# A diffusion trunk layer in fp32: part of a matrix product moved to VectorE, and a new order in the attention

## Chip, cores and metric

One core of a Trainium2 chip. The metric is the device time of one launch in microseconds; lower is better. Engines: TensorE (PE), VectorE (DVE), ScalarE (ACT), GpSimd (POOL), and SyncE (SP), which only issues loads and stores here.

## What is computed

One layer (DEPTH is 1) on 128 context tokens and 256 latent tokens, width 2048, all fp32:

```python
m = silu(cond) @ w_mod + b_mod          # six rows of 2048 for each of two conditions
h = rms_norm(x, n1) * (1 + sc1) + sh1
q, k, v, u = split(h @ w_in)            # 16 heads of 64, and a Fourier part u
attn = softmax(q k^T / 8 + bias) v      # neighbourhood window and context keys
fn = real(fft2(u))                      # over positions and group channels
g_na, g_fn = split(sigmoid(h @ w_gate))
x = x + g1 * ((g_na * (attn @ w_na) + g_fn * (fn @ w_fnet)) @ w_o)
h2 = rms_norm(x, n2) * (1 + sc2) + sh2
x = x + g2 * swiglu(h2, w_gate_up, w_down)
```

Context tokens use the condition c_ctx, latent tokens c. The outputs are both token sets and the context's k and v.

## The kernel before

Every large product is made of three matmuls (mm3, L147 to L149): each fp32 operand is split into a high part H, rounded to fp32r, and a low rest L, and H·H, H·L and L·H are added in PSUM. Weights come in units of 256 rows by 512 columns (load_unit, L185, on SP's queue; four buffers). split_unit (L195) makes wh on ScalarE and wl on VectorE, one unit ahead of PE. The program's order is written out by hand: the units are a fixed list, and next_unit (L208) lets the front work make a step (A), splits the next unit, lets the front and the other work make a step (B), and issues the load of a later unit. In the gate stage, mid_unit makes a third step for the front work halfway through the unit's matmuls (M). A Paced generator (L58) collects its rate at each tick and makes its steps when what it has collected reaches `least`. Ahead (L84) issues loads some items before their use; loads on SP's queue go out in program order, and one that waits for its buffer holds up those behind it.

The stages are these. First the tokens' norm and transposes. Then the projection by w_in, in four groups of k-tiles (GROUPS: k-tile 0, then 1 and 2, then 3 to 6, then 7 to 15), each group running over eight column chunks: 8, 8, 16 and 40 units. Beside it, prepare (L570) computes shift and scale of the first norm for the k-tiles of MODS (one, then five times three): mod_sums (L392) multiplies the 32 columns of csz, of which two hold the conditions, with 128 rows of w_mod at a time (wm, L384, two k-rows a load, four buffers); four such matmuls at column positions 0, 32, 64 and 96 are one step. mod_cols (L416) turns the sums into columns, and modulate (L535) makes the tokens hH and hL of a k-tile. When prepare is through, the stream `rows` starts (with_rows, L605): mod_rows (L306) adds up w_mod's other four parts on VectorE (accr, L329), sums over partitions on PE (L338) into a PSUM bank, and adds the bank to the bias row one step later (L343).

Next is the gate projection, eight times eight units, with the Fourier mix (fourier, L697) and then the attention (L802) as front work, and with `rows`. The Fourier mix calls positions for each group and half, splits the next u, and calls channels. The attention goes pair of heads by pair; the string PAIR gives the calls of each tick, by the table at L992: t0 and t1 transpose probabilities, qk transposes q and k, b adds the mask, lq, lb and lv load, s0 and s1 are the scores, m0 and m1 their maxima, e0 and e1 the exponentials on ScalarE with their sums, i0 and i1 (inverses, L939) the reciprocals on VectorE and the scaling on ScalarE (L944), pv the values, v a split of the values. All of these share the four PSUM banks of at_tile with `rows`; a bank is given again when its last reader has been written into the program. The gate products use the four others.

Then come the two branch projections with the gates (f4, L1081), the output projection (cc, L1170), in which transposed (L1151) makes the next product's operand from finished columns, and the feed-forward part in six rounds.

Of the kernel before, what the change touches and what calls it, by code (L numbers as in the profile page):

```python
# [13 lines left out]
F32 = mybir.dt.float32  # L14
# [5 lines left out]
P = 128  # L20
# [19 lines left out]
GROUPS = [(0, 1), (1, 2), (3, 4), (7, 9)]  # L40
ORDER = [6, 7, 0, 1, 2, 3, 4, 5]
DUE = [-1.4, 0, 0, 0]
PREP = [1.75, 1.8, 1.8, 1.8]
PAIR = "t1 qk,b,,,,lq,s0 s1 m0,e0 i0,m1,pv lb,e1 i1,,t0,v,lv"

# [54 lines left out]
def trunk_kernel(ctx: ExitStack, tc: tile.TileContext, io: dict):  # L102
# [163 lines left out]
    with ExitStack() as ph:  # L266
# [22 lines left out]


        ROWS = (2, 4, 3, 5)

        def row_weights():

# [11 lines left out]
        def mod_rows(ty, src):  # L306


            for cc in range(2):
                acc = rpool.tile([P, 2, 2, CH], F32, tag="acc", name=nm("accr"))  # L310
                row = rpool.tile([P, CH], F32, tag="row", name=nm("row"))
                nc.gpsimd.memset(row, 0.0)
                b = b_mod[ty * D + cc * 2 * CH : ty * D + (cc + 1) * 2 * CH].rearrange("(i n) -> i n", i=2)
                for cnd in range(2):
                    for i in range(2):
                        q = 64 * cnd + 32 * i
                        nc.gpsimd.dma_start(row[q : q + 1], b[i : i + 1])
                for k in range(KT):
                    _, wm = src.take()
                    for cnd in range(2):  # L320
                        if cnd:
                            if ty != ROWS[0] or cc + k:
                                src.more()
                            yield
                        sc = csz[:, k, cnd : cnd + 1]
                        if k == 0:
                            nc.vector.tensor_scalar_mul(acc[:, cnd], wm, sc)
                        else:
                            nc.vector.scalar_tensor_tensor(  # L329
                                out=acc[:, cnd], in0=wm, scalar=sc, in1=acc[:, cnd], op0=ALU.mult, op1=ALU.add  # L330
                            )
                    yield
                yield
                o = rows_psum["tile"]()
                for cnd in range(2):
                    for i in range(2):
                        q = 64 * cnd + 32 * i
                        nc.tensor.matmul(  # L338
                            o[q : q + 32], ones, acc[:, cnd, i], start=True, stop=True,
                            tile_position=(0, q), skip_group_check=True,  # L340
                        )
                yield
                nc.vector.tensor_add(row, row, o)  # L343
                for cnd in range(2):
                    for i in range(2):
                        q = 64 * cnd + 32 * i
                        c0 = (2 * cc + i) * CH
                        nc.gpsimd.dma_start(s_row[ty][cnd][:, c0 : c0 + CH], row[q : q + 1])
# [23 lines left out]
        def depth_of(n):  # L372

            return 4 if n == 1 else 2

        def mod_weights(alloc):


            def load(kt0, n, k0):
                w, nk = n * P, depth_of(n)  # L380
                wm = alloc([P, 2, nk, w], "wm")
                for ty in range(2):
                    col = ty * D + kt0 * P
                    nc.sync.dma_start(  # L384
                        wm[:, ty],
                        w_mod[k0 * P : (k0 + nk) * P, col : col + w].rearrange("(k p) n -> p k n", p=P),
                    )
                return wm

            return Ahead(load, [(kt0, n, k0) for kt0, n in MODS for k0 in range(0, KT, depth_of(n))], 0)  # L390

        def mod_sums(src, kt0, n, alloc, out):  # L392

# [3 lines left out]
            for k0 in range(0, KT, nk):  # L397
                _, wm = src.take()
                for kk in range(0, nk, 2):
# [13 lines left out]
                        out.append(rows)  # L413
                    yield

        def mod_cols(kt0, n, rows):  # L416

            pt = md_tile()
            for j in range(n):
                nc.tensor.matmul(pt[:, j * 4 : j * 4 + 4], rows[:, j * P : (j + 1) * P], sel, start=True, stop=True)  # L420
            m = pt[:, : n * 4].rearrange("p (k i c) -> p k i c", i=2, c=2)
            yield


            def bc(ap):
                return ap.unsqueeze(2).to_broadcast([P, n, 2])

            nc.vector.tensor_add(msh[0][:, kt0 : kt0 + n, :], m[:, :, 0], bc(bcol[:, kt0 : kt0 + n]))
            d = msc[0][:, kt0 : kt0 + n, :]
            nc.vector.tensor_add(d, m[:, :, 1], bc(bcol[:, KT + kt0 : KT + kt0 + n]))  # L430
            nc.vector.scalar_tensor_tensor(
                out=d, in0=d, scalar=1.0, in1=bc(ng[:, 0, kt0 : kt0 + n]), op0=ALU.add, op1=ALU.mult
            )
            yield


        with ExitStack() as pha:
            wmp = phm.enter_context(tc.tile_pool(name="wmp", bufs=4, side="right"))
            cpool = pha.enter_context(tc.tile_pool(name="cpool", bufs=12))
            tmp = pha.enter_context(tc.tile_pool(name="tmpa", bufs=2))  # L440

# [15 lines left out]
                nc.sync.dma_start(t[:, 0, :], xp[:, cc * CH : (cc + 1) * CH])  # L457
                xc.append(t)
            src = mod_weights(wme)
            for _ in range(2):  # L460
                src.more()
            loads = Ahead(load_unit, units, 1)
            for _ in range(2):
                src.more()
            loads.more()

            rows_n = tmp.tile([64, P], F32, tag="rows_n", bufs=1, name="rows_n")
            nc.gpsimd.dma_start(rows_n[0:16], io["norm1_g"][0].rearrange("(k p) -> k p", p=P))
# [101 lines left out]
            def prepare():  # L570

                follow = columns_and_tokens(*MODS[0])
                while prepared[0] < 1:
                    yield next(follow)
                for k0, n in MODS[1:]:
                    for _ in mod_sums(src, k0, n, wme, sums):
                        next(follow, None)
                        yield
                    follow = columns_and_tokens(k0, n)
                    while k0 == 1 and prepared[0] < 3:  # L580
                        yield next(follow)
                for _ in follow:
                    yield

            prep = Paced(prepare())
            rows_psum["tile"] = md_tile

            def rows_and_columns():
# [62 lines left out]

            for gi, (k0, n) in enumerate(GROUPS):
                prep.due, prep.rate = DUE[gi], PREP[gi]
                prep.least = 3.6 if gi else 1
                if gi == len(GROUPS) - 1:
                    behind.append(Paced(expand_rpb(), 0.2))
                    new_ring()
# [39 lines left out]
        def fourier():  # L697
            with ExitStack() as st:
# [8 lines left out]
                def split_table(name, raw):  # L707
                    H, L = (fc.tile(raw.shape, F32R, tag=name + x, name=nm(name + x)) for x in "HL")
                    split(H, L, raw)
                    return H, L  # L710

                def load_u(g):
                    return table([P, NT, FG], s_qkvu[6 + g // 2][:, :, (g % 2) * FG : (g % 2 + 1) * FG])
# [64 lines left out]
                for pair in range(2):  # L778
                    for gi in range(2):
                        for cc in range(2):  # L780
                            positions(gi, cc)
                            yield
                            if pair + gi + cc == 0:
                                chH, chL = split_table("chan", chan)
                            yield
                        if pair + gi < 2:
                            uH, uL = split_table("u", u)
                            yield
                            if pair == 0:
                                u = load_u(gi + 2)  # L790
                        yield
                    if pair:
                        for got, load in ((qks, load_qk), (biases, load_bias), (vs, load_v)):
                            got.append(Ahead(load, [(hp,) for hp in range(8)], 1))
                    for cp in range(2):
                        channels(pair, cp)
                        yield
                        yield
                        yield
# [48 lines left out]
        def attention_pair(hp, wk, rest):  # L848
# [90 lines left out]
            def inverses(qt):  # L939
                sm = t["sm", qt]  # L940
                n = len(halves[qt])
                nc.vector.reciprocal(sm[:, :n], sm[:, :n])
                for i, (j, sl) in enumerate(halves[qt]):
                    nc.scalar.activation(  # L944
                        out=sc[:, j, sl], in_=sc[:, j, sl], func=AF.Copy, scale=sm[:, i : i + 1]
                    )

            def keys_first(qt):

# [198 lines left out]
        rows_until(2)  # L1148
        yield from load_rows(tmpo, 2, cc, "gb", 2)

    def transposed(cc, tile=at_tile):  # L1151

        for k in range(4):
            kt = cc * 4 + k
# [7 lines left out]
            for g, sl in conds:  # L1162
                nc.vector.scalar_tensor_tensor(
                    out=L[:, sl], in0=o[:, sl], scalar=g, in1=fr(H[:, sl]), op0=ALU.mult, op1=ALU.subtract
                )
            yield

    rows.rate = RATES[3]
    xin = [None] * 4
    for cc in range(4):  # L1170
# [3 lines left out]
        for u in range(0, KT, 2):  # L1174
# [7 lines left out]
                shifts(xw, 0)  # L1182
            if u == 2 and cc:
                rows_until(4)
                behind.append(Paced(transposed(cc - 1)))
            for t in range(NT):
                sl = slice(t * P, (t + 1) * P)
                for kk in range(2):
# [55 lines left out]
            yield  # L1244

    norm = Paced(normed(), 1.25, 3)
    behind += [Paced(inverse()), Paced(transposed(3, mm_tile), 1, 1), norm]


    phf = ctx.enter_context(ExitStack())  # L1250
# [162 lines left out]
```

## Time and profile before

| | |
|---|---|
| three runs | 2046.58, 2047.31, 2047.31 us; median 2047.31 |
| the profiled execution | 2046.09 us, span 2044.3 us |
| PE busy | 2022.1 us, 99% |
| VectorE busy | 1244.4 us, 61% |
| ScalarE busy | 758.6 us, 37% |
| DMA over the span | 192 GB/s |
| granted PE clock, mean | 0.997 |

A busy engine is not always at its peak: matmuls are pipelined and their ends are modelled, so PE's share says that the stream has hardly a hole, and the distance from one start to the next says how dense it is. The span is that of the profiled execution; its time is 1.8 us longer, and the median of the runs another 1.2 us.

### The profile page before, as it was taken

To read this page: it belongs to the slowest core of one execution; us is meant where nothing else is said; L and a number is where in the kernel's file an instruction comes from. 1 tells how busy PE (TensorE), PEld (TensorE's weight loads), DVE (VectorE), ACT (ScalarE), POOL (GpSimd) and SP (SyncE) were. 2 spreads that over 40 slices of the span, in tenths; PEclk is the share of its full clock that TensorE was granted. 3 is DMA by queue.
4 is the path that set the end of the run, shared out by engine and by line. 5 is a ranking of instruction groups with operands and counts; after the bars stand their busy time and mean duration, and the time that the engine had idled before them with its cause. 6 is when DMAs were issued, how large, how long until landed. Compare 5 with 4: busy or idle time off the path is not lost.

```text
span 2044.3 us, 27532 instructions
## 1 busy us (share of the span) xinstructions
PE 2022.1 (99%) x10986; PEld 1844.3 (90%) x10986; DVE 1244.4 (61%) x1524; ACT 758.6 (37%) x1139; POOL 43.0 (2%) x92
## 2 busy tenths in 40 slices
PE   7999999999999999999999999999999999999999
PEld 4668888999999999889998999899989998999897
DVE  4746898778988778765844454544454334333456
ACT  5433232456656443334523332222322232323222
POOL 1000000000000000010000000000000000000000
PEclk8999999999999999999999999999999999999999
DMA  9995979677776776754455455444554444444453
GB/s 328 334 338 181 330 261 323 206 224 225 230 209 185 251 245 200 240 189 139 120 169 162 147 156 160 148 155 148 162 155 141 124 127 125 132 124 125 138 161 124
DMA packets 220384, 390.46 MB, mean 191 GB/s; under 512 B 28464, under 2 KB 77632, under 8 KB 220256
## 3 DMA queue, kind: packets, MB, share of 16 engines
q1 hardware_dynamic: 213088, 382.13, 59.5%
q10 hardware_dynamic: 4672, 6.31, 0.8%
q8 instruction: 86, 1.41, 0.3%
q0 software_dynamic: 2496, 0.27, 0.1%
q14 instruction: 42, 0.34, 0.0%
HBM read 371.81 MB, written 20.51 MB: 192 GB/s over the span
## 4 chain that ended last, share of the span: by engine, by line
PE 93%; DMA 3%; DVE 2%; ACT 1%; issue 0%; SPq 0%; ACTq 0%; DVEq 0%
PE mm L147 19%; PE mm L149 19%; PE mm L148 19%; PE at L147 11%; PE at L149 11%; PE at L148 11%; PE at L404 1%; DVE wl L144 1%; DMA wm<-in_w_mod 1%; DMA wraw<-in_w_in 1%; DVE accr L329 1%; DMA xc<-in_x_prompt 0%; PE at L981 0%; PE at L960 0%; PE at L338 0%
## 5 line engine op out<-in xcount | busy, mean ns | idle before, releaser
L144 DVE TENSOR_TENSOR wl<-wraw,wh 128x1024 fp32r<-128x1024 f32 (+1 forms) x464 | 559.1, 1205 | 672.7 <-ACT wh L143 668.9
L143 ACT CAST wh<-wraw 128x1024 fp32r<-128x1024 f32 (+1 forms) x464 | 481.1, 1038 | 1036.8 <-PE at L148 274.1
L147 PE MATMUL mm<-hH,wh 128*128 128x384 f32 x1152 | 387.9, 337 | 0.2 <-ACT gst L1036 0.2
L149 PE MATMUL mm<-hH,wl 128*128 128x384 f32 x1152 | 385.3, 334 | 0.0
L148 PE MATMUL mm<-hL,wh 128*128 128x384 f32 x1152 | 385.2, 334 | 0.0
L329 DVE SCALAR_TENSOR_TENSOR accr<-wmr,csz,accr 128x1024 f32<-128x1024 f32 x240 | 304.2, 1278 | 0.1
L147 PEld LDWEIGHTS mm<-hH,wh 128*128 128x128 f32 x1152 | 216.3, 188 | 5.1 <-issue 4.5
L148 PEld LDWEIGHTS mm<-hL,wh 128*128 128x128 f32 x1152 | 216.3, 188 | 0.0
L149 PEld LDWEIGHTS mm<-hH,wl 128*128 128x128 f32 x1152 | 216.2, 188 | 0.0
L147 PE MATMUL at<-hH,wh 128*128 128x384 f32 x640 | 213.9, 334 | 0.0
L149 PE MATMUL at<-hH,wl 128*128 128x384 f32 x640 | 213.9, 334 | 0.0
L148 PE MATMUL at<-hL,wh 128*128 128x384 f32 x640 | 213.8, 334 | 0.0
L147 PE MATMUL mm<-wh,hH 128*128 128x512 f32 x404 | 160.8, 398 | 1.9 <-ACT hH L548 1.2
L149 PE MATMUL mm<-wh,hL 128*128 128x512 f32 x404 | 158.4, 392 | 0.6 <-DVE hL L144 0.4
L148 PE MATMUL mm<-wl,hH 128*128 128x512 f32 x404 | 158.0, 391 | 0.8 <-DVE wl L144 0.8
L149 PE MATMUL mm<-wh,cL 128*128 128x512 f32 x352 | 137.1, 389 | 0.0
L147 PE MATMUL mm<-wh,cH 128*128 128x512 f32 x352 | 137.0, 389 | 0.0
L148 PE MATMUL mm<-wl,cH 128*128 128x512 f32 x352 | 137.0, 389 | 0.0
L147 PEld LDWEIGHTS at<-hH,wh 128*128 128x128 f32 x640 | 120.1, 188 | 1.0 <-ACT wh L143 0.8
L148 PEld LDWEIGHTS at<-hL,wh 128*128 128x128 f32 x640 | 120.1, 188 | 0.2
L149 PEld LDWEIGHTS at<-hH,wl 128*128 128x128 f32 x640 | 120.1, 188 | 0.0
L147 PEld LDWEIGHTS mm<-wh,hH 128*128 128x128 f32 x404 | 76.1, 188 | 25.6 <-issue 3.1
(282 smaller groups left out, 2631.1 us busy)
## 6 DMA issues: line engine op xcount, KB each, us to landing
wraw<-in_w_gate_up SPq DMA_DIRECT2D x176, 512.0 KB, 3.7
wmr<-in_w_mod SPq DMA_DIRECT2D x128, 512.0 KB, 4.9
wraw<-in_w_down SPq DMA_DIRECT2D x88, 512.0 KB, 3.7
wraw<-in_w_gate SPq DMA_DIRECT2D x64, 512.0 KB, 4.3
wm<-in_w_mod SPq DMA_DIRECT2D x80, 384.0 KB, 6.8
wraw<-in_w_in SPq DMA_DIRECT2D x56, 512.0 KB, 6.2
wraw<-in_w_o SPq DMA_DIRECT2D x32, 512.0 KB, 4.6
wraw<-in_w_fnet_proj SPq DMA_DIRECT2D x16, 512.0 KB, 5.0
```

The source lines that it names most:

```text
L143: nc.scalar.copy(H, x)
L144: nc.vector.tensor_sub(L, x, fr(H))
L147: nc.tensor.matmul(out, aH, bH, start=start, stop=False)
L148: nc.tensor.matmul(out, aH, bL, start=False, stop=False)
L149: nc.tensor.matmul(out, aL, bH, start=False, stop=stop)
L329: nc.vector.scalar_tensor_tensor(out=acc[:, cnd], in0=wm, scalar=sc, in1=acc[:, cnd], op0=ALU.mult, op1=ALU.add)
L404: nc.tensor.matmul(pm[q : q + 32, :w], csz[:, k, :], wm[:, ty, kk + par, :], start=k < 2, stop=k >= KT - 2, tile_position=(0, q), skip_gro ...
```

## The change

The modulations of the last three k-tiles (13 to 15) are computed in two ways. For the first four of 16 k-rows (EARLY) they stay on PE. For the other twelve, late_sums loads 128x384 pieces (wd, five buffers) and adds them up on VectorE, for each condition, in tiles that later hold the tokens of k-tiles 13 and 14; it is paced at 1.5 pieces a unit from the second group on. late_rows then makes the first four k-rows' matmuls and four matmuls with `hot`, whose column of ones sums each accumulator over the partitions into its row of the same bank. prepare's rates in the last two groups fall to 1.6. At the start, all four first wm loads go out ahead of the two w_in units.

In mod_rows, ScalarE copies the sums out of the bank in the tick of its matmuls, and VectorE adds the copy. In the Fourier mix, both halves of a group are called in one tick, the split of the next u follows one tick later, and a group of ticks is one longer. In the attention, i0 and i1 come two ticks after their exponentials, and VectorE does the scaling. In the output projection, transposed does two k-tiles a step at half the rate.

```diff
-PREP = [1.75, 1.8, 1.8, 1.8]
-PAIR = "t1 qk,b,,,,lq,s0 s1 m0,e0 i0,m1,pv lb,e1 i1,,t0,v,lv"
+PREP = [1.75, 1.8, 1.6, 1.6]
+LATE = 1.5
+EARLY = 4
+PAIR = "t1 qk,b,,,,lq,s0 s1 m0,e0,m1,i0 pv lb,e1,,i1 t0,v,lv"
...
+        hot = consts.tile([P, 2, 32], F32, tag="hot", name="hot")
+        nc.vector.memset(hot, 0.0)
+        for cnd in range(2):
+            nc.vector.memset(hot[:, cnd, cnd : cnd + 1], 1.0)
...
+                nc.scalar.copy(acc[:, 0, 0], o)
                 yield
-                nc.vector.tensor_add(row, row, o)
+                nc.vector.tensor_add(row, row, acc[:, 0, 0])
...
+            got = Ahead(load, [(k, ty) for k in range(EARLY, KT) for ty in range(2)], 5)
+            yield
+            for k in range(EARLY, KT):
+                for ty in range(2):
+                    if k + ty > EARLY:
+                        got.more()
+                    _, wd = got.take()
+                    for a, sc in zip(late_acc[ty], (csz[:, k, cnd : cnd + 1] for cnd in range(2))):
+                        if k == EARLY:
+                            nc.vector.tensor_scalar_mul(a, wd, sc)
+                        else:
+                            nc.vector.scalar_tensor_tensor(
+                                out=a, in0=wd, scalar=sc, in1=a, op0=ALU.mult, op1=ALU.add
+                            )
+                    yield
...
+            for ty in range(2):
+                for cnd, a in enumerate(late_acc[ty]):
+                    q = 32 * (2 * ty + cnd)
+                    nc.tensor.matmul(
+                        pm[q : q + 32, :w], hot[:, cnd], a, start=False, stop=True,
+                        tile_position=(0, q), skip_group_check=True,
+                    )
...
-            for _ in range(2):
+            for _ in range(4):
                 src.more()
-            loads = Ahead(load_unit, units, 1)
-            for _ in range(2):
-                src.more()
-            loads.more()
+            loads = Ahead(load_unit, units, 2)
...
-                for k0, n in MODS[1:]:
+                for k0, n in MODS[1:-1]:
...
-                for _ in follow:
+                prep.least = 1
+                yield from follow
+                while late.live:
+                    late.step()
                     yield
+                late_rows(*MODS[-1], wme, sums)
+                yield
+                yield from columns_and_tokens(*MODS[-1])
...
-                prep.least = 3.6 if gi else 1
+                prep.least = 3.6 if gi in (1, 2) else 1
+                if gi == 1:
+                    behind.append(late)
...
                         for cc in range(2):
                             positions(gi, cc)
-                            yield
-                            if pair + gi + cc == 0:
-                                chH, chL = split_table("chan", chan)
-                            yield
+                        yield
                         if pair + gi < 2:
                             uH, uL = split_table("u", u)
+                        yield
+                        if pair + gi == 0:
+                            chH, chL = split_table("chan", chan)
+                        yield
+                        if pair == 0:
+                            u = load_u(gi + 2)
+                        for _ in range(3):
                             yield
-                            if pair == 0:
-                                u = load_u(gi + 2)
-                        yield
...
-                    nc.scalar.activation(
-                        out=sc[:, j, sl], in_=sc[:, j, sl], func=AF.Copy, scale=sm[:, i : i + 1]
-                    )
+                    nc.vector.tensor_scalar_mul(sc[:, j, sl], sc[:, j, sl], sm[:, i : i + 1])
...
-    def transposed(cc, tile=at_tile):
+    def transposed(cc, tile=at_tile, each=2):
...
-            yield
+            if k % each == each - 1:
+                yield
...
-                behind.append(Paced(transposed(cc - 1)))
+                behind.append(Paced(transposed(cc - 1), 0.5))
...
-    behind += [Paced(inverse()), Paced(transposed(3, mm_tile), 1, 1), norm]
+    behind += [Paced(inverse()), Paced(transposed(3, mm_tile, 1), 1, 1), norm]
```

## Rows read from the trace of the kernel before

**Rows 1.** Page, busy time: engine, us, share of the span, instructions.

```profile
PE 2022.1 (99%) x10986; PEld 1844.3 (90%) x10986; DVE 1244.4 (61%) x1524; ACT 758.6 (37%) x1139; POOL 43.0 (2%) x92
```

**Rows 2.** PE's waits over the whole run: total us, times, longest us.

```profile
PE at L865 <- DVE row L343: 1.2, 1, 1.2
...
PE at L865 <- DVE pt L144: 0.9, 1, 0.9
...
PE at L149 <- DVE uL L144: 0.9, 1, 0.9
...
PE at L404 <- DMA wm<-in_w_mod: 0.4, 2, 0.2
```

**Rows 3.** Chain in order of time, last modulation group: start us, us, what.

```profile
137.83 0.78 PE at L404 x8
...
139.38 2.07 PE at L404 x24
141.45 0.43 PE mm L147
141.88 0.23 PE mm L148
...
149.83 2.72 PE at L404 x32
```

**Rows 4.** Stretches of 5 us: busy us (instructions) by engine, PE clock, DMA share, GB/s.

```profile
60.00:65.00 5.00, 5.00 (x37) 2.83 (x36) 4.92 (x8) 2.45 (x4) 0.00 (x0) 1.00 0.75 200
65.00:70.00 5.00, 5.00 (x24) 4.13 (x22) 3.26 (x5) 1.06 (x1) 0.00 (x0) 1.00 1.06 376
...
95.00:100.00 5.00, 5.00 (x36) 3.38 (x29) 3.04 (x5) 3.99 (x9) 0.00 (x0) 1.00 0.88 288
...
115.00:120.00 5.00, 5.00 (x43) 2.57 (x42) 1.54 (x4) 2.33 (x4) 0.00 (x0) 1.00 0.88 244
```

**Rows 5.** Stretches: the saturated part of the first stage, and attention.

```profile
56.00:152.00 96.00, 95.55 (x575) 65.64 (x578) 54.80 (x80) 35.60 (x55) 0.00 (x0) 1.00 0.99 336
...
420.00:670.00 250.00, 247.78 (x1590) 240.16 (x1589) 208.91 (x276) 154.79 (x345) 9.69 (x20) 1.00 0.73 213
```

**Rows 6.** Page, DMA issues: count, KB each, median us to landing.

```profile
wm<-in_w_mod SPq DMA_DIRECT2D x80, 384.0 KB, 6.8
wraw<-in_w_in SPq DMA_DIRECT2D x56, 512.0 KB, 6.2
```

**Rows 7.** Groups by line: VectorE by form, 420 to 665 us; then L944 of the page.

```profile
L869 DVE SCALAR_TENSOR_TENSOR qL<-at,qg,qH 128x384 fp32r<-128x384 f32 x8 | 4.9, 609 | 0.0
...
L327 DVE TENSOR_SCALAR accr<-wmr,csz 128x1024 f32<-128x1024 f32 x4 | 2.9, 745 | 0.0
...
L944 ACT ACTIVATE sc<-sc,sm 128x384 f32<-128x384 f32 (+1 forms) x48 | 22.7, 536 | 4.9 <-DVE sm L942 4.9
```

**Rows 8.** Chain in order of time at the longest wait of PE at L865.

```profile
482.96 0.61 DVE row L343
...
483.62 0.44 PE at L865 x2
```

**Rows 9.** Groups by form, 0 to 200 us: VectorE at L547, ScalarE at L678.

```profile
L547 DVE TENSOR_SCALAR hf<-xT,msc,msh 128x256 f32<-128x256 f32 x1 | 0.4, 407 | 0.0
...
L678 ACT COPY acc<-mm 128x512 f32<-128x512 f32 x16 | 9.2, 586 | 11.1 <-PE mm L149 10.6
```

**Rows 10.** VectorE's waits, 420 to 665 us: total us, times, longest us.

```profile
DVE pt L144 <- ACT pt L143: 15.8, 12, 3.3
DVE wl L144 <- ACT wh L143: 7.0, 15, 1.7
DVE sm L942 <- ACT sc L934: 5.0, 5, 2.2
DVE sc L907 <- PE at L895: 4.9, 3, 3.0
DVE aT L990 <- ACT lo L989: 3.7, 9, 1.4
```

More of the change, by code (lines that the diff above doesn't have):

```diff
@@ L291, in trunk_kernel @@
         ROWS = (2, 4, 3, 5)
+        late_acc = []
+        hot = consts.tile([P, 2, 32], F32, tag="hot", name="hot")
+        nc.vector.memset(hot, 0.0)
+        for cnd in range(2):
+            nc.vector.memset(hot[:, cnd, cnd : cnd + 1], 1.0)
         def row_weights():
@@ L388, in load @@
                 return wm
-            return Ahead(load, [(kt0, n, k0) for kt0, n in MODS for k0 in range(0, KT, depth_of(n))], 0)
+            return Ahead(load, [(kt0, n, k0) for kt0, n in MODS
+                for k0 in range(0, KT if kt0 < MODS[-1][0] else EARLY, depth_of(n))], 0)
         def mod_sums(src, kt0, n, alloc, out):
@@ L414, in mod_sums, with late_sums, load, late_rows @@
                     yield
+        def late_sums(kt0, n):
+            w = n * P
+            def load(k, ty):
+                wd = wdp.tile([P, w], F32, tag="wd", name=nm("wd"))
+                c0 = ty * D + kt0 * P
+                nc.sync.dma_start(wd, w_mod[k * P : (k + 1) * P, c0 : c0 + w])
+                return wd
+            for ty in range(2):
+                late_acc.append(
+                    [hpool.tile([P, w], F32, tag=f"t{c}{KT - 3 + ty}", name=nm("late")) for c in "HL"]
+                )
[14 more added lines that the diff above has]
+                    yield
+        def late_rows(kt0, n, alloc, out):
+            w = n * P
+            pm = at_tile()
+            for k in range(0, EARLY, 2):
+                _, wm = src.take()
+                for ty in range(2):
+                    for par in range(2):
+                        q = 32 * (2 * ty + par)
+                        nc.tensor.matmul(
+                            pm[q : q + 32, :w], csz[:, k + par, :], wm[:, ty, par, :], start=k == 0, stop=False,
+                            tile_position=(0, q), skip_group_check=True,
+                        )
+            for ty in range(2):
+                for cnd, a in enumerate(late_acc[ty]):
+                    q = 32 * (2 * ty + cnd)
+                    nc.tensor.matmul(
+                        pm[q : q + 32, :w], hot[:, cnd], a, start=False, stop=True,
+                        tile_position=(0, q), skip_group_check=True,
+                    )
+            rows = alloc([P, w], "mrow")
+            nc.scalar.copy(rows, pm[:, :w])
+            out.append(rows)
         def mod_cols(kt0, n, rows):
@@ L438, in trunk_kernel @@
             wmp = phm.enter_context(tc.tile_pool(name="wmp", bufs=4, side="right"))
+            wdp = phm.enter_context(tc.tile_pool(name="wdp", bufs=5, side="right"))
             cpool = pha.enter_context(tc.tile_pool(name="cpool", bufs=12))
@@ L581, in prepare @@
                         yield next(follow)
-                for _ in follow:
+                prep.least = 1
+                yield from follow
+                while late.live:
+                    late.step()
                     yield
+                late_rows(*MODS[-1], wme, sums)
+                yield
+                yield from columns_and_tokens(*MODS[-1])
             prep = Paced(prepare())
+            late = Paced(late_sums(*MODS[-1]), LATE)
             rows_psum["tile"] = md_tile
```

## The prediction, made before the change was run

> **What bounds the kernel now.** Read the busy table first: TensorE (PE) is busy 99% of the 2044.3 us span [rows 1], so only two things can shorten the kernel: instructions taken from PE's stream, and the moments at which PE stands still. Then read PE's waits over the whole run [rows 2]: they are few and short. Three lie in the gate stage, where the Fourier mix and the attention run beside the gate projection: 0.9 us for uL, 1.2 and 0.9 us at L865, each once. Then the chain in order of time over the first stage, where the modulations (L404) interrupt the projection [rows 3], and then the table by stretches, for the engines that could become late: DMA [rows 4, 5] and VectorE [rows 5].
>
> The first stage has two limits at once. Between 56 and 152 us PE is busy 95.6 of 96 us while DMA is busy 0.99 of the time [rows 5]. So what is taken from PE there counts only as far as the weights arrive. In the attention stretch, 420 to 670 us, PE is busy 247.8 of 250 us, VectorE 208.9 and ScalarE 154.8 [rows 5]; there a shift from ScalarE to VectorE has 41 us of room, unless VectorE's own waits use it.
>
> **Part 1: modulations of the last three k-tiles.** Before, they are 8 ticks of 8 instructions on PE (4 matmuls of two passes). They take 0.78 (x8), 2.07 (x24) and 2.72 us (x32) [rows 3], or 0.65 us for each further 8, with 0.13 us at each start; the first projection matmul after a block takes 0.43 us where 0.23 is usual, so a block costs 0.33 us besides its ticks. After, two k-pairs (16 instructions) and the four sums over partitions (8 of the same shape) make one block of 24. Five ticks fall away, 5 x 0.65 = 3.2 us. Counting the ticks of prepare() at its old and new rates, the blocks from the second group on go from nine to eight: 0.3 us more. Sum: **-3.6 us**, all of it on PE's path if the loads keep up.
>
> The loads: the same bytes of w_mod are read, but as 24 pieces of 192 KB (half of a 384 KB load [rows 6]) on SP's one queue, five of them at the first unit of the second group, the others one or two a unit, ahead of each unit's w_in load. So they come earlier than the wm loads they replace. By my count, before the last k-pair of k-tiles 10 to 12 lands, which PE takes about 122 us, 18 pieces come in addition, and one w_in load of 512 KB less: 3.5 - 0.5 = 3.0 MB. At the 376 GB/s of a full stretch this is 8.0 us of DMA. The cover is DMA that stands open: 60 to 65 us moves 200 GB/s, 95 to 100 us 288, 115 to 120 us 244 [rows 4], short of 376 by 2.3, 1.2 and 1.8 us, and the shallower dips between them may give some 1.5. So the cover is some 6.8 us and PE waits **+1.2 us**. The bounds are 0 (all dips fill) and 8.0 - 2.3 = 5.7 us (only the lull at 60 us fills, because dips between loads come from SP waiting for buffers and may come again). I stay near the lower end: the five pieces go out without a wait, exactly into that lull, and the queue is fuller afterwards.
>
> VectorE pays 48 more passes of 128x384: 44 scalar_tensor_tensor, 0.61 us by L869's row of the same shape, though it reads PSUM [rows 7], and 4 cheaper ones, 29 us in all. From 56 to 152 us it is busy 54.8 of 96 [rows 5]; with 29 more, 84. I cost it at nothing: wl is split one unit ahead, and its idle time there is room. If a burst delays wl, the w_in load behind it on SP's queue starts later too, as do the pieces; that is inside the 5.7. SP gets 12 more issues. The rows' stream starts one unit later, which leaves its deadlines whole by the same count. The three memsets for hot and the order of the first loads (four wm loads, then two units) lie before the first projection matmul; what it wins on wm, ScalarE's cast of the later w_in unit takes back: 0, within 0.2 either way.
>
> **Part 2: the gate stage.** The row's bank is now emptied by ScalarE in the tick of its matmuls. Before, it was held until a later tick's VectorE add, so that the next transposes had three banks instead of four. The 1.2 us is the wait for that add itself: row, then PE [rows 8]; the 0.9 us for pt follows when the ring is one short, since k's transposes must take the bank that t1 has just filled. Both go: -2.1. The split of u moves from one unit to two units ahead of positions(): the 0.9 us for uL goes. Sum **-3.0 us**, bounds 0 and -3.3 (with the idle before the weight load). The copy costs ScalarE 8 x 0.59 us (L678, the same shape, [rows 9]); it makes ScalarE wait until PE reaches the sums, with the next cast of wh queued behind it. ScalarE has some 95 of 250 us free there [rows 5]; I take 0.
>
> The scales: 48 activations of 0.54 us leave ScalarE, 22.7 us [rows 7], none on PE's path. On VectorE the nearest rows are L547, 0.41 us at 256 columns [rows 9], and L327, 0.75 at 1024 [rows 7]; the scales average 299 columns, so 0.42 us each, 20 us; bounds 48 x 0.28 = 13 (L327 scaled down) and 48 x 0.61 = 29 (L869). VectorE then has 208.9 + 20 = 229 of 250 us.
>
> What hides these 20 us: the waits that VectorE has now. Its reciprocal waits 5.0 us for the exponentials just issued [rows 10]; two ticks later they are done. The extra Fourier tick also puts attention's steps behind the unit's split rather than ahead of it, so that wl no longer queues behind evacuations that wait for PE. Against that, locally VectorE will be near full, so some unit may come late: **+0.5 us**, bounds 0 and the rival below.
>
> **Part 3.** Two transposes in one tick, and two positions(), save entries into PE's stream; a few of the 0.1 us kind: **-0.2 us**, bounds 0 and -0.6. PE's order against DMA does not change there.
>
> Sum: -3.6 + 1.2 - 3.0 + 0.5 - 0.2 = -5.1 us. The profiled execution took 2046.1 us (span 2044.3 and 1.8 around it), so 2041.0 by that; the median is 1.2 us above it, 2047.3: I predict **2042.2 us**.
>
> **The rivals.** (1) VectorE becomes the bound in attention and the kernel is slower. Its waits there for pt, wl, sc and aT are 15.8 + 7.0 + 4.9 + 3.7 = 31.4 us [rows 10]. If they stay, 229 + 31.4 = 260.4 us must pass where 250 did. It decides from the point at which more than 21 of the 31.4 remain. All of them: +10.4 in place of -2.1 and +0.5, so 2047.3 - 3.6 + 1.2 - 0.9 - 0.2 + 10.4 = 2054.2. For it: VectorE is already the busier engine. Against it: it is at 84% and not full, and pt and wl wait for ScalarE, which loses 22.7 us of work. 0.08. The Trainium skill ("Perfetto Trace Analysis", Optimizing Scalar/DVE Operations) advises giving work to ScalarE when VectorE is saturated; the change does the reverse, and by that rule this rival would be the likely one. The trace of before does not bear the rule's condition out. (2) DMA binds in the first stage: +5.7 in place of +1.2, 2046.7. For it: DMA at 0.99 [rows 5]. Against: PE waits only 0.4 us for wm in the whole run [rows 2]. 0.20. (3) The bank stalls only move, because the ring of four banks is as tight with VectorE later: nothing of the 3.0, 2045.2. For it: the wait for pt was one of VectorE's speed, not of the row alone. 0.16.
>
> **How the numbers follow.** The forecast, with its own range 2039.5 to 2044.0, has 0.56; rivals 0.08, 0.20, 0.16. A measurement here can tell about 0.2%, 4.1 us, from no change: faster means under 2043.2. Of the forecast 0.47 lies there, and 0.08 of rivals 2 and 3 in their milder forms: 0.55. Slower, over 2051.4, is rival 1 with a little more: 0.08. The same: 0.37. The range runs from 2038.8 (all covers hold, both upper gains) to 2047.2, which takes in rivals 2 and 3.
>
> **What would show it.** Right: L404 with 344 instructions instead of 384, one block of 24 for the last group near 145 us, no PE wait for wm above 1.5 us, no wait at L865 or for uL, VectorE near 229 us of some 247 between 420 and 670 us without a PE wait on wl. Wrong: PE waiting for wm between 70 and 130 us (rival 2); waits of PE for wl, pt or sc after 430 us (rivals 1 and 3); an L144 on wl that ends after PE's last matmul of the unit before. A prediction of this kind fails if two streams that are both full, DMA and PE before 152 us, collide in a way that their averages do not show.

## The result, and the profile after

The change makes the kernel slower by 0.16%: 2049.73 us, median of 20 runs, against 2046.47 us for the kernel before on the same chip; the ratio is 1.0016, with a 95% interval from 1.0009 to 1.0022. The forecast was 2042.2 us, and the range ended at 2047.2; its base of 2047.3 was the median of only the first three of the 20 runs of the kernel before. Less is lost than the 0.2% that the prediction called measurable, but it is lost where 5.1 us of gain were expected.

The page of the changed kernel: PE is as full as before [rows 1], and its span is 3.5 us longer.

```profile
span 2047.8 us, 27557 instructions
...
PE 2021.7 (99%) x10946; PEld 1843.8 (90%) x10946; DVE 1284.3 (63%) x1629; ACT 740.7 (36%) x1093; POOL 44.0 (2%) x92
```

PE's waits over the whole run, the rows that answer to [rows 2] (total us, times, longest us). The waits at the row's bank (L865, now L936) and for uL are gone. New are one of 2.1 us for the last sum of a row on VectorE, and four kinds beside the attention (L1029 twice, L1047, and L345 for pt):

```profile
PE at L345 <- DVE accr L336: 2.1, 1, 2.1
PE at L483 <- ACT mrow L421: 2.0, 3, 0.9
PE at L1029 <- DVE sc L1015: 1.8, 2, 1.4
...
PE at L413 <- DMA wm<-in_w_mod: 0.9, 3, 0.4
...
PE at L345 <- DVE pt L146: 0.7, 1, 0.7
...
PE at L1029 <- ACT sc L1005: 0.4, 1, 0.4
PE mm L149 <- DVE acc L752: 0.4, 1, 0.4
...
PE at L1047 <- ACT sc L987: 0.2, 1, 0.2
```

Waits alone don't say where 3.5 us come from. For that, both traces were cut at the same points of the program, the first projection matmul of the unit with which a stage begins:

| stage (units) | before, us | after, us | difference |
|---|---|---|---|
| start to the last group (0 to 31) | 181.97 | 179.84 | -2.13 |
| last group of the projection (32 to 71) | 148.11 | 148.22 | +0.11 |
| gate stage: Fourier mix, attention (72 to 135) | 340.06 | 340.55 | +0.49 |
| branch projections, "mix" (136 to 167) | 134.35 | 139.22 | **+4.87** |
| output projection (168 to 199) | 137.66 | 137.49 | -0.17 |
| feed-forward and end | 1102.18 | 1102.50 | +0.32 |

Each number is that of one execution. How far it can be off shows where several kernels of this document share a stage's program. The stretch up to the last group took 181.4 to 183.0 us in three traces with the old first stage (mean 182.1) and 178.9 to 181.3 in eleven with the new (mean 180.0). The changed gate stage with the stream in its new place took 340.02, 340.55 and 341.01 us. The mix, where PE waits for nothing in it, took 134.35 to 134.55 us. So the first and the fourth line are clear of this spread, and the gate stage's +0.49 is not.

So the first stage won about what was forecast, the gate stage won nothing, and the mix, in which the diff changes nothing but one copy, lost more than all of it. There the timeline shows one spot. Before (start us, us, engine, line), the partition sums of a row start 6.1 us after the start of the row's last sum on VectorE, which takes 1.28, and run in one piece of 1.06 us:

```profile
738.97 1.28 DVE L329 SCALAR_TENSOR_TENSOR accr<-wmr,csz,accr 128x1024 f32<-128x1024 f32 x1
...
745.11 1.06 PE L338 MATMUL at<-accr,ones 128*32 128x512 f32 x8
```

After, PE reaches the second half of them before VectorE has made the last sum, which stands behind a split of wl:

```profile
747.92 1.05 PE L345 MATMUL at<-accr,ones 128*32 128x512 f32 x4
...
748.61 1.23 DVE L146 TENSOR_TENSOR wl<-wraw,wh 128x1024 fp32r<-128x1024 f32 x1 [0.39 <-ACT wh L145]
...
749.75 1.28 DVE L336 SCALAR_TENSOR_TENSOR accr<-wmr,csz,accr 128x1024 f32<-128x1024 f32 x1
...
751.08 1.92 PE L345 MATMUL at<-accr,ones 128*32 128x512 f32 x4 [2.11 <-DVE accr L336]
```

And PE comes back from the wait at half its clock. Stretches of 1 us (busy us of PE, PEld, DVE, ACT, POOL; granted clock; DMA share; GB/s):

```profile
750.00:751.00 1.00, 0.00 (x0) 0.00 (x0) 1.00 (x2) 0.89 (x1) 0.00 (x0) 1.00 0.73 301
751.00:752.00 1.00, 0.92 (x4) 0.19 (x4) 1.00 (x2) 0.00 (x0) 0.00 (x0) 0.51 0.76 270
752.00:753.00 1.00, 1.00 (x5) 0.07 (x1) 0.16 (x1) 0.00 (x0) 0.00 (x0) 0.50 0.86 264
753.00:754.00 1.00, 1.00 (x4) 1.00 (x4) 0.00 (x0) 0.59 (x1) 0.00 (x0) 0.50 0.70 213
754.00:755.00 1.00, 1.00 (x6) 1.00 (x6) 0.04 (x1) 0.00 (x0) 0.00 (x0) 0.78 0.88 254
```

Why the distance shrank can be read in the code. `rows` makes its steps by a rate; between the last sum and the partition sums lies one empty step, so normally two ticks. When a tick makes two steps, it can be one. Which row meets such a tick depends on the stream's phase, and `rows` starts later than before, because prepare ends a unit later. By the order of the instructions the stream is 1.5 steps behind when the mix begins: with 1.5 steps given to it, each of its instructions stands again in the unit that it had before. The traces agree: from the second on, five partition sums start on PE in the units 76, 99, 122, 153 and 187 before, in 77, 100, 123, 154 and 189 after, and in the old units again in e9 below, where the steps are given back.

### The profile page after: what moved, and what is told of

It is laid out like the page before. It is cut to its first block, busy times and chain, and to the rows that moved or that the text cites. A ratio compares the mean times of both kernels' runs of the same rounds, so it can differ in the third digit from the quotient of the medians.

```text
span 2047.8 us, 27557 instructions
## 1 busy us (share of the span) xinstructions
PE 2021.7 (99%) x10946; PEld 1843.8 (90%) x10946; DVE 1284.3 (63%) x1629; ACT 740.7 (36%) x1093; POOL 44.0 (2%) x92
## 3 DMA queue, kind: packets, MB, share of 16 engines
q8 instruction: 86, 1.41, 0.3%
## 4 chain that ended last, share of the span: by engine, by line
PE 70%; DVE 0%; issue 0%; ACT 0%; ACTq 0%
PE mm L149 13%; PE mm L150 13%; PE mm L151 13%; PE at L149 10%; PE at L150 10%; PE at L151 10%; PE at L345 0%; PE at L1050 0%; PE at L1226 0%; PE at L1029 0%; PE at L966 0%; DVE x L1427 0%; DVE d L1426 0%; PE mm L1226 0%; DVE wl L146 0%
```

## Experiments

Each ratio is to the kernel before, run beside it on the same chip. Its medians lie between 2046.0 and 2046.5 us, so where runs of different chips are compared, some 0.4 us of the difference can be the chip's.

**The stream's phase.** The first theory: the loss in the mix is one of phase. Rival: it is ScalarE's new copy, which waits for PE ahead of a cast of wh. e1 gives the steps back to the changed kernel, e2 takes them from the kernel before, both at the start of the mix.

```diff
         rows.rate = RATES[2]
+        rows.due += 1.5        # e1, on the changed kernel; e2: rows.due -= 1.5, on the kernel before
```

> The changed kernel with one line added at the start of the mix stage: the paced rows' stream is given 1.5 steps in advance, so that from there on its sums over k and its partition sums (L345) stand in the same units as in the kernel before. Theory 'phase': in the changed kernel L345 follows its last VectorE sum one unit later instead of two, waits 2.1 us for it at 749 us, and PE then runs some units at the lower clock. Given back its old place, L345 takes about 1.0 us as before, no PE wait stands there, the clock stays at 1.00, and the kernel takes 4.7 us less than the changed one: about 2045.0 us, 1.5 us under the kernel before. Rival 'copy': ScalarE's copy of the bank, which waits for PE ahead of the next cast of wh, is what costs; then moving the stream changes the place of the loss but not its size, and the kernel stays within 1.5 us of 2049.7.

> The kernel before with one line added at the start of the mix stage: the rows' stream loses 1.5 steps, so that its sums and partition sums stand in the same units as in the changed kernel; VectorE still empties the bank (no copy on ScalarE), and nothing else of the change is made. Theory 'phase': L338 waits about 2 us for the last VectorE sum near 750 us and the granted clock falls after it; the kernel takes 4 to 5 us more than before, about 2051. Rival 'copy': without ScalarE's copy the loss is at most the bare wait of 2.1 us, about 2048.5. Rival 'elsewhere': the phase does not matter in the kernel before, 2046.5.

e1: 2049.13 us, ratio to before 1.0015 (1.0005 to 1.0024). The wait at 749 us is gone, but the time is hardly better, 0.6 us under the changed kernel: the steps given in advance put sums of 1.28 us in front of the splits of the attention's output on VectorE, the bank of the first branch's products is read late, and PE waits for it (PE's waits from 300 to 800 us):

```profile
PE mm L149 <- DVE gl L1167: 2.9, 1, 2.9
PE at L1029 <- DVE sc L1015: 1.4, 1, 1.4
```

e2: 2050.79 us, ratio 1.0020 (1.0011 to 1.0030). The old kernel has the new kernel's wait, without any copy on ScalarE:

```profile
PE at L338 <- DVE accr L329: 2.1, 1, 2.1
PE at L865 <- DVE row L343: 1.2, 1, 1.2
```

Its mix stage takes 137.45 us, 3.1 more than before, at a clock of 1.00 throughout: 2.1 us of wait, and 1.0 because the partition sums run in two pieces of 1.05 us, on either side of the wait, instead of one of 1.06. So the phase makes the wait, and the copy isn't needed for it; the 1.8 us that the changed kernel's mix loses beyond these 3.1 come where its clock stands at 0.50.

The same steps, given in the second quarter of the mix instead (e5):

```diff
             gl = [None, None]
+            rows.due += 1.5 * (f4 == 1)
```

> The changed kernel; the rows' stream gets its 1.5 steps back at the second quarter of the mix stage (f4 = 1) instead of at its start, where the run before this one (steps given at the start) took the wait at 749 us away but put a new wait of 2.9 us at 688 us, behind the split of the attention's output on VectorE. Theory 'phase': neither wait stands, the clock stays at 1.00, and the kernel takes about 4.7 us less than the changed one: 2045.0, span 2043.1. Rival 'crowding': VectorE is so full in this stage that the steps given in advance push another of PE's needs late wherever they are put, and the kernel stays at 2047 or more.

2045.09 us, ratio 0.9995 (0.9986 to 1.0004): 4.6 us less than the changed kernel, as expected (4.3 by the distances from the kernel before). The mix takes 134.51 us, and PE waits nowhere in it.

**Each part alone.** e7 is Part 1 with the gate stage, row add and transposes of the kernel before, and the line of e5. e8 is Part 2 alone (PAIR, the Fourier mix's order, the scales, the copy) on the kernel before.

> Part 1 of the change alone: the late sums on VectorE, their rates and the order of the first loads, on the gate stage, row add and transposes of the kernel before; the rows' stream gets its 1.5 steps back in the second quarter of the mix, so that it stands there as before. Theory: what the first stage won by the traces (PE 2.2 us ahead from 160 us on) reaches the end: about 2044.1. Rival 'the rows' stream loses it elsewhere': in the gate stage, where it stands 1.5 steps later than before, other waits appear and take 1 us or more of it, 2045 to 2047.

> Part 2 of the change alone on the kernel before: new order of the attention's ticks and of the Fourier mix, scales on VectorE, ScalarE empties the row's bank. The first stage and the rows' stream are those before. Theory 'a stall for a stall': the waits of 0.9, 1.2 and 0.9 us at uL, the bank and pt go, new ones of about 3 us at L1029 and at the partition sums come: within 1 us of before, 2045.3 to 2047.3. By the prediction's term (3.0 us won, 0.5 paid): 2043.8.

e7: 2050.13 us, ratio 1.0022 (1.0013 to 1.0031), the rival's side and beyond it. Its first stage has its gain (179.98 us), but its gate stage takes 346.77 us instead of 340.06, with two waits of 2 us for banks, both at instructions of `rows`:

```profile
PE at L368 <- DVE pt L146: 2.1, 1, 2.1
PE at L345 <- DVE pt L146: 1.9, 1, 1.9
PE at L151 <- DVE uL L146: 0.8, 1, 0.8
```

The same kernel with the 1.5 steps given back at the start of the gate stage (e11):

```diff
         rows.rate = RATES[1]
+        rows.due += 1.5
```

> Part 1 of the change alone, as in the run before (which took 2050.1 with waits of 1.9 us at the partition sums at 481 us and 2.1 us at a column transpose at 631 us), but with the rows' stream given its 1.5 steps back at the start of the gate stage. Theory 'phase': both waits go, no new ones come, and the 2.2 us of the first stage reach the end: about 2044.0. Rival 'the old gate stage does not go with the new first stage for another reason' (another order on ScalarE or SP at the border): waits of that size stay, 2047 or more.

2045.21 us, ratio 0.9995 (0.9986 to 1.0004); gate stage 340.46 us. Those two waits are gone, the old ones of the bank are back:

```profile
PE at L934 <- DVE pt L146: 0.9, 1, 0.9
PE at L934 <- DVE row L350: 0.7, 1, 0.7
```

So moving one stream by one and a half steps is worth 4.9 us in this kernel (e7 against e11), and it decides whether Part 1 is a loss of 4 us or perhaps a gain of 1, which the interval of e11 does not tell from nothing.

e8: 2045.21 us, ratio 0.9995 (0.9986 to 1.0005). The gate stage takes 339.76 us, 0.30 less than before, which is within the spread of one execution (the same old gate stage took 340.47 in e2): a stall for a stall, as that theory said. PE's only waits of the gate stage are now these two, near 446 and 654 us:

```profile
PE at L960 <- DVE sc L946: 1.8, 2, 1.3
```

**The parts of the gate stage.** e3 is e1 with the copy undone (VectorE adds from the bank a step later). e4 is e1 with the scales on ScalarE again, in the new ticks:

```diff
-                    nc.vector.tensor_scalar_mul(sc[:, j, sl], sc[:, j, sl], sm[:, i : i + 1])
+                    nc.scalar.activation(out=sc[:, j, sl], in_=sc[:, j, sl], func=AF.Copy, scale=sm[:, i : i + 1])
```

> e1 with ScalarE's copy of the row's bank undone: VectorE adds the row straight from the bank a step later, as before the change. Theory 'the stalls were given back by the scales': the stalls at the bank (1.2 and 0.9 us in the kernel before, near 482 and 601 us) are partly back, since they came from the bank held until a later step: 1 to 2 us over e1, with PE waiting for the row's add near 482 or 601 us. Rival 'the copy costs': ScalarE waits for PE in front of a cast of wh at all eight copies, and taking it out wins 0.5 to 2 us against e1.

> e1 with the scales of the probabilities back on ScalarE (48 activations), in the new order of ticks. Theory 'late scales': what the gate stage lost (PE waiting at L1029 1.45, 0.4 and 0.4 us for scales and exponentials, in place of the 3.0 us of stalls that went) comes from VectorE, which issues the scales behind wl and wl behind ScalarE's cast; with them on ScalarE the three waits go or shrink below 0.5 us in all, and the kernel takes 1.5 to 2.5 us less than e1, about 2043. Rival 'ScalarE is as late': the scales stand behind the next exponentials on ScalarE and wait for VectorE's reciprocal, casts of wh come later, and the kernel takes the same as e1 or up to 2 us more.

e3: 2050.57 us, ratio 1.0022 (1.0013 to 1.0032), 1.4 over e1; the two intervals overlap. The gate stage takes 341.24 us, 1.2 us longer than in e1 (0.2 longer than in e5, which has e1's gate stage), with a wait of 1.0 us for a bank at L935 near 481 us that neither of them has. So the copy removes that wait; what it is worth in time is not clear of the spread. (The mix is 1.3 us longer too; that is the clock, see the end.)

e4: 2065.96 us, ratio 1.0097 (1.0081 to 1.0112). My theory fell. Instead of a gain of 2 us it lost 17, all in the gate stage (357.25 us). PE now waits 16 times for ScalarE's scales at the transposes of probabilities:

```profile
PE at L1031 <- ACT sc L1015: 7.4, 16, 1.6
```

All of PE's listed waits in that stage come to 12.0 us, against 2.6 in e1. That is 9 of the 17 us. A part of the rest falls into 3 us at half the clock near 448 us; the remainder doesn't stand as waits in the trace.

In the new ticks the scales must be on VectorE. e12 asks the reverse, whether copy and Fourier order do without both; it is the changed kernel with the old PAIR, the scales on ScalarE, and the 1.5 steps given at the start of the gate stage.

> Of the gate stage's changes only ScalarE's copy of the row's bank and the order of the Fourier mix; the scales are on ScalarE and the ticks in the order of the kernel before. First stage and transposes as in the changed kernel, rows' stream given its 1.5 steps back at the start of the gate stage. Theory 'the scales ate it': the copy and the order win what the prediction said, 3.0 to 3.3 us in the gate stage (336.8 instead of 340.06 between the first units of the gate and the mix stage), and VectorE's scales in the new ticks were what paid it back (they leave 339.76 there): 2041.0 in all, faster than every kernel so far. Rival 'the copy needs the new ticks': in the old order ScalarE has 22.7 us more, its copy waits for PE in front of exponentials and casts, new waits come and the gate stage takes 339 us or more: 2043.5 or above.

2047.21 us, ratio 1.0005 (0.9996 to 1.0014), gate stage 343.19 us: the rival, by its number. The wait for uL is gone, but PE waits three times for the bank of a pt, once for 2.1 us:

```profile
PE at L933 <- DVE pt L146: 3.4, 3, 2.1
```

The cause that the rival named, the copy, is not what this longest wait shows: near 569 us VectorE's pt stands behind its wl, that waits for ScalarE's cast, and the cast stands behind ScalarE's scales, which had waited 1.41 us for VectorE's reciprocals.

So the edits of the gate stage don't add up. Copy and order alone lose 3.1 us there, the new ticks without VectorE's scales 17, and all together win 0.3.

**Better versions.** The changed kernel with the line of e11 at the start of the gate stage (e9), and besides it one exponential of a single column ahead of the attention (e10):

```diff
         def attention():
+            warm = small.tile([P, 1], F32, tag="warm", bufs=1, name=nm("warm"))
+            nc.scalar.activation(out=warm, in_=ones[:, 0:1], func=AF.Exp)
```

> The changed kernel; the rows' stream gets its 1.5 steps back at the start of the gate stage, so that in the gate, the mix and all later stages its sums and partition sums stand in the units of the kernel before. Theory 'phase everywhere': besides the wait at 749 us also those that PE has in the gate stage near 554 to 602 us (0.66 before the values, 0.40, 0.62 at L345), which the gate part alone did not have, go. First stage 2.2 us won, gate stage 0.3 won (by the gate part alone), nothing lost after: span near 2042, 2043.6 us. Rival 'the gate's stalls are the scales' own': they stay with the stream in its old place, and the time equals that of the run with the steps given back in the mix, about 2045.

> The run with the rows' steps given back from the gate stage on, and besides it one exponential of a single column at the start of attention, so that ScalarE's table load of 1.28 us, which stands in front of the first pair's exponentials at 440 us, comes earlier. Theory 'late scales by a late cast': the wait of 1.4 us at L1029 at 445 us comes from VectorE's scales queued behind wl, wl behind ScalarE's cast, and the cast behind table load and exponentials; with the load out of that chain the wait shrinks to 0.2 us or goes: 1.2 us less than the run without it, about 2042.4. Rival 'the ticks are too close': VectorE is late there for its own work, the wait keeps at least 1 us, and the time stays the same.

e9: 2044.01 us, ratio 0.9990 (0.9981 to 0.9999), faster than the kernel before and 5.7 us faster than the changed one. Its stages are the sum of the parts: 179.67 us to the last group, gate stage 339.76, mix 134.35. From 300 to 800 us PE has these waits left:

```profile
PE at L1029 <- DVE sc L1015: 1.7, 2, 1.2
```

The longer of them stands in the changed kernel at 445 us, in the first pair of heads. ScalarE loads its table for the exponential there, so the exponentials and the cast of wh behind them come late, VectorE waits for that cast, and its scales stand behind it:

```profile
440.24 1.28 ACT L1005 ACT_TABLE_LOAD   x1
...
443.52 1.04 ACT L145 CAST wh<-wraw 128x1024 fp32r<-128x1024 f32 x1
...
444.59 1.23 DVE L146 TENSOR_TENSOR wl<-wraw,wh 128x1024 fp32r<-128x1024 f32 x1 [1.65 <-ACT wh L145]
...
445.94 1.14 DVE L1015 TENSOR_SCALAR sc<-sc,sm 128x384 f32<-128x384 f32 x4
...
446.50 1.22 PE L1029 MATMUL at<-ident,sc 128*128 128x128 f32 x8 [1.45 <-DVE sc L1015]
```

The Trainium skill ("ScalarE activation tables: per-element evaluation and per-set limits", What a function is on this engine) puts functions of two sets one table load of 1283 ns apart; the trace agrees (1.28 us). In e10 the load falls at 426 us, before the attention, and the wait shrinks from 1.24 to 0.70 us, less than forecast. The gate stage gives 0.87 us more (338.89), the median only 0.14, too little to tell from nothing: 2043.87 us, ratio 0.9988 (0.9979 to 0.9997). What stays is VectorE's own queue: from wl to the scales it has no pause there.

The last attempt at these waits (e6) takes e5 and puts t0 one tick later:

```diff
-PAIR = "t1 qk,b,,,,lq,s0 s1 m0,e0,m1,i0 pv lb,e1,,i1 t0,v,lv"
+PAIR = "t1 qk,b,,,,lq,s0 s1 m0,e0,m1,i0 pv lb,e1,,i1,t0 v,lv"
```

> The run with the rows' steps given back in the second quarter of the mix, and besides it t0 (the first transposes of the probabilities) one tick after i1 (the second scales), in the tick of v, as the kernel before had them apart. Theory 'late scales': PE's waits at L1029 (1.45 us at 445 us, 0.4 each near 505 and 560) come from t0 reaching PE before VectorE has scaled; a tick later they go, 1.5 to 2.2 us less than the run without it, about 2043. Rival 'the pair is full': the next pair's t1 and qk then follow t0 closely and wait for banks or for pt's splits; same time or up to 2 us more.

2045.50 us, ratio 1.0001 (0.9991 to 1.0010), against 2045.09 without it; the gate stage is 0.83 us longer. PE no longer waits for scales and waits for banks instead, four times, as the rival said:

```profile
PE at L933 <- DVE pt L146: 3.6, 4, 1.2
```

## Why the prediction was wrong

**The step that failed** is a sentence of Part 1: "The rows' stream starts one unit later, which leaves its deadlines whole", costed at nothing. The deadlines are whole; no wait of PE for a finished row stands in the list above. But a paced stream has a second property, where its steps fall beside the other engines' work. 1.5 steps cost 4.87 us in the mix (2.1 of wait, 1.0 for the sums in two pieces, 1.8 at the lower clock) and 0.79 in the gate stage (340.55 against 339.76 us in e9; 0.3 to 1.2 with the gate stages of e1 and e5). That is 5.7 us, the same as the medians give (2049.73 against 2044.01), or 5.3 by the distances from the kernel before on each chip. With the stream in its old place the change is what I had called it, a gain, and its 2044.01 us lie inside the range, though it is 2 us and not 5. Of the 3 us that are still short, 2 are Part 2's.

**Part 1** was forecast at -3.6 + 1.2 = -2.4 us and measured -2.13, 2.2 by the means; that the two are so close is luck, for the second term was wrong. The -3.6 was right: 320 instructions at L413 and one block of 24 for the last group, 344 as counted, and one block fewer from the second group on. That group in order of time, at 152 us instead of my 145:

```profile
152.35 1.50 PE L464 MATMUL at<-wm,csz 128*32 128x384 f32 x16
...
153.66 0.83 PE L471 MATMUL at<-late,hot 128*32 128x384 f32 x8
...
158.65 0.73 PE L483 MATMUL at<-sel,mrow 128*128 128x4 f32 x6
```

The columns of this last group, the third line, come alone in both kernels; the chain of before has them too:

```profile
160.93 0.56 PE at L420 x6
```

DMA's +1.2 did not come: PE waits 0.9 us for wm instead of 0.4 [rows 2], but all of it before 60 us and none where I had put it; DMA's share from 56 to 152 us fell from 0.99 to 0.96. Two other waits, which I had not counted, came in its place. At 139 us the columns follow directly on their own sums, where before eight instructions of the next sums lay between, and PE waits for ScalarE's copy of the sums:

```profile
139.20 0.83 PE L483 MATMUL at<-sel,mrow 128*128 128x4 f32 x6 [0.60 <-ACT mrow L421]
```

And VectorE's 29 us, measured at 44 x 0.61 + 4 cheaper ones, were not free: four late sums in a row stood in front of the add that empties a bank, and PE waited 0.38 us.

```profile
99.96 2.20 DVE L450 SCALAR_TENSOR_TENSOR late<-wd,csz,late 128x384 f32<-128x384 f32 x4
102.07 1.88 DVE L752 TENSOR_TENSOR acc<-acc,mm 128x512 f32<-128x512 f32 x3
...
102.81 0.50 PE L149 MATMUL mm<-wh,hH 128*128 128x512 f32 x1 [0.38 <-DVE acc L752]
```

So -3.6 + 0.6 + 0.4 = -2.6 us. The third group of the projection (units 16 to 31), where nearly all of this lies, took 81.4 to 81.7 us in the three traces with the old first stage and 78.8 to 79.2 in the eleven with the new: 2.5 us less.

**Part 2** was forecast at -3.0 + 0.5. The three waits did go, as said. What was mis-sized is the +0.5, the price of later scales. With the stream in its old place the stage wins 0.30 us, so about 2.7 us came back (2.3 against the 340.47 us of e2): 1.7 as waits for scales at L1029, while the rest doesn't stand as waits in the trace, and its cause stays open. Rival 3, the stalls only move, was the right one; its cause was named wrongly (the ring of banks), though e6 shows that the ring is what waits next. The scales themselves were dearer in the forecast than on the chip:

```profile
L1015 DVE TENSOR_SCALAR sc<-sc,sm 128x384 f32<-128x384 f32 (+1 forms) x48 | 15.1, 372 | 0.6
420.00:670.00 250.00, 246.86 (x1580) 238.08 (x1579) 221.85 (x328) 133.53 (x293) 10.19 (x20) 1.00 0.70 209
```

15.1 us busy and not 20 (0.37 us each and not 0.42, and they overlap), and VectorE is busy 221.9 us of 250 (third engine of the row) where I had 229 [rows 5]. The average was never the question: the wait in the first pair comes from one cast on ScalarE that VectorE's queue waits for. ScalarE's copy was costed at nothing, and no loss by it shows (e3 against e1).

**Rival 1**, VectorE as the bound, didn't happen: its waits for pt [rows 10] are gone, and it waits longer for ScalarE's casts of wh (20.9 us between 420 and 670 us, 7.6 before), without PE waiting for wl there. The Trainium skill ("Perfetto Trace Analysis", Optimizing Scalar/DVE Operations) says that offloading work to ScalarE may make sense when VectorE is saturated. That condition is not met here (221.9 of 250 us), and e4, which moves the scales that way all the same, loses 17 us. **Rival 2**, DMA, didn't happen either: PE waits nowhere for wm between 60 and 180 us. **Part 3**: the output projection won 0.1 to 0.2 us, as forecast.

The prediction's own tests found a part of it: no wait at L936 or for uL, none over 1.5 us for wm, one block of 24 are all there, while "waits of PE for wl, pt or sc after 430 us" was named as the sign of trouble and came (3.1 us in five waits). No test named the mix, since no term stood for it.

**Open.** The eleven kernels with Part 1 take some 0.3 us more from the feed-forward stage to the end (1102.50 against 1102.18), after VectorE's last add; why was not tried.

## What to carry to other kernels

When work is paced by rates, an edit that makes one stream end later shifts the phase of the next stream through every later stage; align the two programs unit by unit and compare where each step of that stream falls, not only whether it meets its deadline. Before judging a change, restore the phase of what it didn't mean to touch: here one line turned a loss of 3.3 us into a gain of 2.0. And look at several traces of the same stage before calling a difference of less than 1 us a gain or a loss. Where the bound engine already stands still for only a few us in all, the waits that an edit removes can come back, as in e8, e6 and e12, at the next ring of buffers or the next queue, so look for the instruction that waits second, and expect edits of one stage not to add up.

## What the hardware showed

The granted clock of PE falls from 1.00 to 0.50 (1.2 instead of 2.4 GHz) for some 3 us after some waits of 1.5 to 3 us and not after others. It fell after waits of 1.59 us (e4, near 445 us), 1.91 and 2.07 (e7), 2.11 (changed kernel), 2.13 (e12) and 2.84 us (e3); it stayed after 1.45 us (changed kernel, 445 us), 2.09 (e2), 2.70 (e4, in the mix) and 2.91 us (e1). e3 and e1 have the same wait at the same place of the program. A stretch of 1 us behind it, in e3 (five matmuls):

```profile
694.00:695.00 1.00, 1.00 (x5) 1.00 (x4) 1.00 (x2) 0.50 (x1) 0.00 (x0) 0.50 0.00 0
```

and in e1 (eight):

```profile
694.00:695.00 1.00, 1.00 (x8) 1.00 (x7) 1.00 (x2) 0.00 (x0) 0.00 (x0) 1.00 0.00 0
```

Their mix stages take 139.04 and 137.72 us, so the fall comes with 1.3 us here; in the changed kernel the mix takes 1.8 us more than in e2, which has its wait without the fall. A wait of 2 us on the bound engine can thus cost nearly twice its length (2.1 + 1.8 us), which a sum of waits doesn't show. What decides whether the clock falls is not shown by these runs.
